# Interleaving the output projection with half of the first feed-forward column group, and loading the residual rows two tiles ahead

## The chip, the core and the metric

The kernel runs on one core of a Trainium2 chip. A core has a matrix engine (PE, whose weight loads are listed as PEld), a vector engine (DVE), a scalar engine (ACT), a general engine (POOL) and a sequencer that mostly issues transfers (SP). Each engine works through its own list of instructions in order; engines wait for each other by semaphores. Transfers (DMA) are issued from SP, ACT or POOL and share 16 DMA engines. The metric is the device time of one execution in microseconds (us). Before the change it is 2557.62 us, the median of three runs (2555.13 to 2560.41).

## The reference

One encoder layer over 2048 tokens of width 1024, in float32: a normed input goes through one input projection, half of the result through dilated attention and half through a gated unit, and then:

```python
    mix = jnp.concatenate([attn, sgu], axis=-1) @ w_out
    x = x + rms_norm(mix, g_post_mix)
    h = rms_norm(x, g_pre_ffn)
    f = jnp.square(jax.nn.relu(h @ w_ff1)) @ w_ff2
    return x + rms_norm(f, g_post_ffn)
```

`w_out` is 1024 x 1024, `w_ff1` 1024 x 4096, `w_ff2` 4096 x 1024. The change lies where the product with `w_out` ends and the feed-forward part begins.

## The kernel before, in words

Each float32 operand is split into a high and a low part (`split_sbuf`, L53, `split_psum`, L73), and each product is three matmuls of 128 x 128 by 128 x 512 that accumulate in one PSUM bank (`mm3`, L82: lines L84, L85, L86). Stage 1 is the input projection, stage 2 the attention with the gated unit's matmuls as filler on PE, and stage 3 the rest. The gated half of `w_out` is multiplied in stage 2 already; its product lies in DRAM as `part`. What is left for stage 3 is the attention half of `w_out`, whose pieces (`c.wo`, 8 pieces of 128 x 512) fill all 8 buffers of the weight pool `c.wp` when stage 2 ends.

Stage 3 begins with the output projection, a loop over 16 tiles of 128 tokens (L923). For tile i:

- `operand` (L889): the attention output `fa` and its reciprocal denominators `fr` (two transfers, each spread over 64 partitions) are loaded by SP, multiplied on POOL (L900), and split on ACT and DVE (L59, L60) into `mh` and `ml`. Operands are asked for two tiles ahead.
- `rest` (L904): the residual rows `r` (from `part`, 512 KB, L907) and `xt` (from x, 512 KB, L909), one tile ahead. There are 3 buffers for `r` and 2 for `xt`.
- 24 matmuls into two banks `mo` (L933), each added to its half of `r` by DVE (L938).
- `post` (L912): the mean square of `r` on ACT (L853) and POOL (L90, L91), the gain on DVE (L914), `xt` added on DVE (L915), and `r` stored to DRAM as `x1d` by a transfer that ACT issues (L916).
- for tiles 0 to 7, one tile later, `prep` (L858): the mean square again, `r` normed **in place** on ACT (L865), 8 transposes on PE into `tp` (L872, tile i's are called tp(i) below), and the split of these into `hh` and `hl` (L75, L76), the operand h of the feed-forward part for tokens 0 to 1023.

Norming `r` in place overwrites what the store of `x1d` reads, so L865 waits until that transfer has landed. On ACT's list the store of tile i+1 stands behind the norming of tile i.

Then comes the feed-forward part, in two halves of 1024 tokens, each with 8 groups of 512 columns of `w_ff1`. `ff1` (L961) takes a group in two passes of 96 matmuls (4 banks `f`, 8 row blocks of weights, 3 matmuls each), squares the result and splits it into `fh` and `fl`; `ff2` (L985) multiplies by 512 rows of `w_ff2` (banks `g`). The first group's `w_ff1` pieces are asked for in tile 15 (L936), since `c.wp` is taken by `c.wo` until then.

Order: the program is written as the loops say, and a scheduler then sets the order of each engine's list by its own priorities. Stage 2's PE and ACT lists are fixed by hand (`in_order`, L35). Pools that begin in stage 3 lie where pools of stage 2 lay; a tile in such a place waits for the last reader and writer of what was there. The pools `s3o` and `s3m` of the output projection are on the right side of the memory, where stage 2 had first its query and key tiles (free early) and next to them the pool `fk`, which is used until the last `w_out` piece is split and the last rows of `part` (tile `ot`, L712, stored by L713) have gone out.

## Time and profile before

| what | value |
| --- | --- |
| time, median of 3 runs | 2557.62 us |
| time of the profiled execution | 2554.44 us |
| its span, first to last instruction | 2552.5 us |
| PE busy | 2398.6 us, 94% of the span |
| DVE, ACT, POOL busy | 1071.2, 935.1, 506.7 us |
| mean granted TensorE clock, share of full speed | 0.972 |
| first matmul of the output projection | 1000.44 us |
| first matmul of the first ff2 (bank g) | 1182.20 us |

The profiled execution is 3.18 us below the median and lies 0.69 us under the lowest of the three runs; 1.94 us of it lie outside the span. Times below are us from the span's start. PE's busy share counts a matmul's whole length, and matmuls overlap, so how far PE is ahead is read from the start times of consecutive ones. Of the idle time before an instruction the profile names what ended it. A transfer is listed where it is issued; "to landing" is the time from there until its semaphore.

### The profile page before, as it was taken

The numbers are of one execution on the slowest core, as the hardware profiler recorded it, in microseconds if no ns is written. First come the engines' busy times: TensorE is split into PE (matmuls) and PEld (weight loads), VectorE is DVE, ScalarE is ACT, GpSimd is POOL, SyncE is SP. The second block draws the span as 40 slices with busy tenths as digits, with TensorE's granted clock in tenths as the row PEclk, the third lists the DMA queues.
The fourth block names the chain that finished last, engine by engine and source line by source line (L and its number), as shares of the span: only waits on it lengthen the run. The fifth ranks groups of instructions, "written<-read, shape, count | busy, mean of one in ns | idle before, by whom it ended". The sixth has DMA issues, their size and how long they took to land.

```text
span 2552.5 us, 31514 instructions
## 1 busy us (share of the span) xinstructions
PE 2398.6 (94%) x11591; PEld 2004.2 (79%) x11591; DVE 1071.2 (42%) x2246; ACT 935.1 (37%) x2053; POOL 506.7 (20%) x553
## 2 busy tenths in 40 slices
PE   8999999888799896689999999999999999999998
PEld 6787887677687785568888888888788888888887
DVE  5524523466666554562223323332731332233325
ACT  4424422366667573433312221222632122112212
POOL 4103103434333222431100100110210011001101
PEclk9999999998899898899999999999999999999999
DMA  7635465667767555772112111111521111111113
GB/s 275 223 121 193 149 173 173 169 161 169 186 173 179 142 154 168 218 260 91 50 34 66 46 50 38 58 46 49 181 93 46 41 54 50 46 50 50 50 42 124
DMA packets 221054, 296.14 MB, mean 116 GB/s; under 512 B 37089, under 2 KB 128740, under 8 KB 217828
## 3 DMA queue, kind: packets, MB, share of 16 engines
q1 hardware_dynamic: 214724, 273.15, 36.5%
q10 hardware_dynamic: 4640, 16.79, 1.7%
q0 software_dynamic: 1536, 4.20, 0.6%
q8 instruction: 91, 1.49, 0.2%
q14 instruction: 63, 0.52, 0.1%
HBM read 216.04 MB, written 78.55 MB: 115 GB/s over the span
## 4 chain that ended last, share of the span: by engine, by line
PE 73%; DMA 14%; DVE 4%; POOL 3%; ACT 3%; issue 2%; SPq 1%; POOLq 0%; DVEq 0%; ACTq 0%
PE f L84 10%; PE f L85 10%; PE f L86 10%; PE g L86 8%; PE g L84 8%; PE g L85 8%; PE mm L85 3%; PE mm L86 3%; PE mm L84 3%; DMA od<-lo 2%; DMA r<-part 2%; DMA lo<-acc 2%; PE t L588 1%; DMA v<-vd 1%; DMA x1d<-r 1%
## 5 line engine op out<-in xcount | busy, mean ns | idle before, releaser
L85 PE MATMUL f<-hh,wl 128*128 128x512 f32 x1024 | 398.5, 389 | 1.9 <-DVE wl L57 1.9
L84 PE MATMUL g<-wl,fh 128*128 128x512 f32 x1024 | 399.0, 390 | 0.0
L85 PE MATMUL g<-wh,fl 128*128 128x512 f32 x1024 | 398.6, 389 | 0.0
L86 PE MATMUL g<-wh,fh 128*128 128x512 f32 x1024 | 398.5, 389 | 0.0
L86 PE MATMUL f<-hh,wh 128*128 128x512 f32 x1024 | 398.4, 389 | 0.0
L84 PE MATMUL f<-hl,wh 128*128 128x512 f32 x1024 | 398.3, 389 | 0.0
L981 POOL TENSOR_TENSOR sq<-sq 128x512 f32<-128x512 f32 x128 | 132.1, 1053 | 1159.7 <-ACT sq L980 1159.7
L56 ACT ACTIVATE wh<-wraw,gain 128x512 fp32r<-128x512 f32 x200 | 143.3, 724 | 504.3 <-PE g L86 423.1
L57 DVE SCALAR_TENSOR_TENSOR wl<-wraw,gain,wh 128x512 fp32r<-128x512 f32 x200 | 157.9, 797 | 267.5 <-ACT wh L56 266.8
L60 DVE TENSOR_TENSOR fl<-sq,fh 128x512 fp32r<-128x512 f32 x128 | 99.1, 775 | 394.8 <-ACT fh L59 386.0
L85 PEld LDWEIGHTS f<-hh,wl 128*128 128x128 f32 x1024 | 192.3, 188 | 42.2 <-DVE wl L57 2.3
L84 PEld LDWEIGHTS f<-hl,wh 128*128 128x128 f32 x1024 | 192.3, 188 | 39.9
L86 PEld LDWEIGHTS g<-wh,fh 128*128 128x128 f32 x1024 | 192.3, 188 | 39.8
L86 PEld LDWEIGHTS f<-hh,wh 128*128 128x128 f32 x1024 | 192.3, 188 | 39.8
L85 PEld LDWEIGHTS g<-wh,fl 128*128 128x128 f32 x1024 | 192.3, 188 | 39.6
L84 PEld LDWEIGHTS g<-wl,fh 128*128 128x128 f32 x1024 | 192.3, 188 | 39.6
L1008 DVE TENSOR_TENSOR acc<-g,acc 128x512 f32<-128x512 f32 x192 | 127.3, 688 | 165.0 <-PE g L86 165.0
L577 ACT ACTIVATE p<-p,m 128x256 f32<-128x256 f32 (+2 forms) x384 | 173.9, 459 | 19.3 <-DVE m L549 19.3
L980 ACT ACTIVATE sq<-f 128x512 f32<-128x512 f32 x128 | 74.8, 597 | 289.2 <-PE f L86 281.9
L60 DVE TENSOR_TENSOR wl<-wraw,wh 128x512 fp32r<-128x512 f32 x144 | 101.8, 708 | 171.2 <-ACT wh L59 169.9
L59 ACT CAST wh<-wraw 128x512 fp32r<-128x512 f32 x144 | 89.5, 622 | 189.2 <-PE f L86 173.5
L525 DVE CUSTOM_DVE_ANT_0 p<-s,bias 128x256 f32<-128x256 f32 (+2 forms) x384 | 120.9, 355 | 42.7 <-PE s L509 32.0
(157 smaller groups left out, 4223.5 us busy)
## 6 DMA issues: line engine op xcount, KB each, us to landing
wraw<-in_w_ff_dram SPq DMA_DIRECT2D x256, 256.0 KB, 2.7
wraw<-in_w_in_dram SPq DMA_DIRECT2D x72, 256.0 KB, 2.7
xt<-in_x_dram SPq DMA_DIRECT2D x32, 512.0 KB, 5.4
v<-vd SPq DMA_DIRECT2D x40, 256.0 KB, 7.0
v<-vd SPq DMA_DIRECT2D x8, 1088.0 KB, 7.9
hd<-ht ACTq DMA_DIRECT2D x16, 512.0 KB, 5.1
vd<-vt SPq DMA_DIRECT2D x16, 512.0 KB, 3.1
qd<-e SPq DMA_DIRECT2D x32, 256.0 KB, 2.8
```

What stands on the lines that cost most here:

```text
L56: nc.scalar.activation(hi, src, AF.Copy, scale=scale)
L57: nc.vector.scalar_tensor_tensor(lo, src, scale, f32(hi), ALU.mult, ALU.subtract)
L59: nc.scalar.copy(hi, src)
L60: nc.vector.tensor_tensor(lo, src, f32(hi), ALU.subtract)
L84: nc.tensor.matmul(out, lhsT=lh, rhs=rl, start=start, stop=False)
L85: nc.tensor.matmul(out, lhsT=ll, rhs=rh, start=False, stop=False)
L86: nc.tensor.matmul(out, lhsT=lh, rhs=rh, start=False, stop=stop)
L525: nc.vector.tensor_tensor_reduce(po, so, bo, -1.0, 1e38, ALU.add, ALU.min, o.nm[:, br, cc:cc + 1])
L577: nc.scalar.activation(p[:, at + lo:at + hi], p[:, at + lo:at + hi], AF.Exp, bias=o.m[:, br, cc:cc + 1], scale=-1.0, accum_out=o.dn[:, br, ...
L980: nc.scalar.activation(sq, b, AF.Relu)
L981: nc.gpsimd.tensor_tensor(sq, sq, sq, ALU.mult)
L1008: nc.vector.tensor_tensor(av, b, av, ALU.add)
```

## The change

The first group of the feed-forward part for tokens 0 to 1023 is cut in two column halves of 256. The first half's 96 matmuls are done in two units of 48, one for tokens 0 to 511 (asked for from tile 5 on) and one for tokens 512 to 1023 (from tile 9 on), put between the matmuls of the output projection. Their weights are loaded as pieces of 128 x 256 into tiles of their own (`first`), the first 8 in tiles 1 to 4, those of the second half in tiles 13 to 15. The second half's 96 matmuls follow the loop, as before.

Beside this: `r` has 4 buffers and `xt` 3, and both are asked for two tiles ahead; the pool of `r` moves to the right side; the gain rows `gmix` and `gpost` share one buffer, so that `gpost` is loaded behind the loop; the tiles `fh` and `fl` lie in two pools of 2 instead of one of 5; `post` is no longer held back for the last three tiles; the first `w_ff2` pieces (`load2(0)`) are asked for behind the loop.

```diff
-        gpost = bcast_row(nc, cst, a["g_post_ffn"][0:1], D, "gpost")
...
+        fpa = ctx.enter_context(tc.tile_pool(name="s3f", bufs=2))
+
+        def ff1_unit(h, ws, c0, es, fs, pool):
+
+            hh, hl = h
+            bs = [pm.tile([P, 512], F32, name=f"f{m}", tag="mm3") for m in range(2 * len(es))]
+            for kc in range(8):
+                wh, wl = ws[kc]
+                for m, b in enumerate(bs):
+                    k, e = divmod(m, len(es))
+                    cs = slice(c0 + k * P, c0 + (k + 1) * P)
+                    ts = slice(es[e] * 512, (es[e] + 1) * 512)
+                    mm3(nc, b, wh[:, cs], wl[:, cs], hh[:, kc, ts], hl[:, kc, ts], kc == 0, kc == 7)
+                yield
+            for k in range(2):
+                if len(fs) == k:
+                    fs.append(tuple(pool.tile([P, 1024], F32R, name=x, tag=x) for x in ("fh", "fl")))
+                fh, fl = fs[k]
+                for e in range(len(es)):
+                    ts = slice(es[e] * 512, (es[e] + 1) * 512)
+                    sq = wk.tile([P, 512], F32, name="sq", tag="sq")
+                    nc.scalar.activation(sq, bs[k * len(es) + e], AF.Relu)
+                    nc.gpsimd.tensor_tensor(sq, sq, sq, ALU.mult)
+                    split_sbuf(nc, sq, fh[:, ts], fl[:, ts])
...
-            op = octx.enter_context(tc.tile_pool(name="s3o", bufs=1, side="right"))
-            om = octx.enter_context(tc.tile_pool(name="s3m", bufs=3, side="right"))
-            orp = octx.enter_context(tc.tile_pool(name="s3r", bufs=3))
-            gmix = bcast_row(nc, op, a["g_post_mix"][0:1], D, "gmix")
+            op = octx.enter_context(tc.tile_pool(name="s3o", bufs=8, side="right"))
+            rctx = octx.enter_context(ExitStack())
+            om = rctx.enter_context(tc.tile_pool(name="s3m", bufs=3, side="right"))
+            orp = rctx.enter_context(tc.tile_pool(name="s3r", bufs=4, side="right"))
+            gmix = bcast_row(nc, cst, a["g_post_mix"][0:1], D, "gmix", "gain")
+
+            def first(kc, pr):
+
+                raw = wk.tile([P, 512], F32, name="wraw", tag="wraw", bufs=c.nraw)[:, 0:256]
+                nc.sync.dma_start(raw, w1[kc * P:(kc + 1) * P, pr * 256:(pr + 1) * 256])
+                wh = op.tile([P, 256], F32R, name="w1h", tag="w1h")
+                wl = op.tile([P, 256], F32R, name="w1l", tag="w1l")
+                split_sbuf(nc, raw, wh, wl, c.gffn[:, kc:kc + 1])
+                return wh, wl
...
-                xt = wk.tile([P, D], F32, name="xt3", tag="xt3")
+                xt = wk.tile([P, D], F32, name="xt3", tag="xt3", bufs=3)
...
-            rx = [rest(0)]
-            old = []
+            rx = [rest(i) for i in range(near)]
+            old, wa, wb, fs0 = [], [], [], []
             for i in range(16):
                 if i + ahead < 16:
                     ops.append(operand(i + ahead))
-                if i + 1 < 16:
-                    rx.append(rest(i + 1))
+                if i + near < 16:
+                    rx.append(rest(i + near))
+                if 1 <= i < 5:
+                    wa += [first(kc, 0) for kc in range(2 * i - 2, 2 * i)]
                 (mh, ml), (r, xt) = ops.pop(0), rx.pop(0)
+                if i in (5, 9):
+                    unit = ff1_unit(h, wa, 0, (i // 9,), fs0, fpa)
+                steps = {5: 3, 6: 3, 7: 3, 9: 2, 10: 2, 11: 2, 12: 3}.get(i, 0)
                 for n in range(2):
...
                     nc.vector.tensor_tensor(r[:, ns], b, r[:, ns], ALU.add)
-                late.append((i, r, xt))
-                if i < 13:
-                    post(*late.pop())
+                    for _ in range((steps + 1 - n) // 2):
+                        next(unit, None)
+                post(i, r, xt)
...
+                if i >= 13:
+                    wb += [first(kc, 1) for kc in range(len(wb), (3, 6, 8)[i - 13])]
+            rctx.close()
+            v0 = load2(0)
+            fpb = ctx.enter_context(tc.tile_pool(name="s3g", bufs=2))
+            fs1 = []
+            for _ in ff1_unit(h, wb, 0, (0, 1), fs1, fpb):
+                pass
+
+        gpost = bcast_row(nc, cst, a["g_post_ffn"][0:1], D, "gpost", "gain")
```

What this does to the order on the engines is shown at three places; the number behind a tile's name tells it from others of that name. First SP's list where stage 2 ends and stage 3 begins, before the change: `od` is the attention output in DRAM, `rd` the denominators, `wraw` a raw piece of `w_out`, `ot` the last rows of `part`.

```order
L894 DMA fa_10020<-od_90 128x4x128
L713 DMA part_87<-ot_9812 128x512
L894 DMA fa_10030<-od_90 128x4x128
L894 DMA fa_10044<-od_90 128x4x128
...
L66 DMA wraw_9961<-in_w_out_dram 128x512
L897 DMA fr_10021<-rd_91 64x4x128
L897 DMA fr_10031<-rd_91 64x4x128
L897 DMA fr_10045<-rd_91 64x4x128
L909 DMA xt3_10056<-in_x_dram 128x1024
L713 DMA part_87<-ot_9967 128x512
L907 DMA r_10040<-part_87 128x1024
L907 DMA r_10054<-part_87 128x1024
```

Here the loads of the first three `fa` stand among the last transfers of stage 2, and the second halves of the first three `fr` directly behind the last `w_out` piece. The same place after the change:

```order
L66 DMA wraw_9961<-in_w_out_dram 128x512
L946 DMA xt3_10047<-in_x_dram 128x1024
L946 DMA xt3_10061<-in_x_dram 128x1024
L713 DMA part_87<-ot_9967 128x512
L920 DMA wraw_10114<-in_w_ff1_dram 128x256
L920 DMA wraw_10204<-in_w_ff1_dram 128x256
L931 DMA fa_10021<-od_90 128x4x128
L934 DMA fr_10022<-rd_91 64x4x128
L931 DMA fa_10031<-od_90 128x4x128
L934 DMA fr_10032<-rd_91 64x4x128
L944 DMA r_10041<-part_87 128x1024
L944 DMA r_10045<-part_87 128x1024
```

(Of four `w_ff1` pieces and of two transfers for each `fr`, one or two rows stand.) All loads of `fa` and `fr` are now behind the last store of `part` and behind four `w_ff1` pieces. The semaphores of `fa_10021` name the landing of that last store, the split of `wraw_9961` on DVE and the last matmul of stage 2's filler: the tile lies where the pool `fk` was.

Last, PE's list from the transposes of tile 2 to those of tile 3 after the change, with the first rows of the first feed-forward unit (`f0`, `f1`) behind them:

```order
L871 MATMUL tp3_10338<-ident_58,r_10059 128x128 x4
L871 MATMUL tp3_10345<-ident_58,r_10059 128x128 x4
L85 MATMUL mo_10450<-wh_9914,ml_10274 128x512
L86 MATMUL mo_10450<-wh_9923,mh_10273 128x512
L871 MATMUL tp3_10422<-ident_58,r_10110 128x128 x4
L871 MATMUL tp3_10429<-ident_58,r_10110 128x128 x4
L84 MATMUL f0_10464<-hl3_10006,w1h_10116 128x512
L85 MATMUL f0_10464<-hh3_10005,w1l_10117 128x512
L84 MATMUL f1_10465<-hl3_10006,w1h_10116 128x512
```

(Of the five matmuls of `mo_10450` between the two, the first and the last stand.) Before, 28 matmuls of `mo` stood between these two groups of transposes. From here to the transposes of tile 7 the list has all 48 matmuls of the first unit; behind those of tile 7 it has 156 of `mo` (129 before) and all 48 of the second unit; the 96 of the second column half follow. The number of PE instructions is the same as before, and from the first ff2 on the lists of PE are the same.

## Rows read from the trace of the kernel before

**Rows 1.** By stretch: us; PE, PEld, DVE, ACT, POOL busy; granted clock; DMA share; GB/s.

```profile
1030.00:1106.00 76.00, 56.93 (x244) 45.49 (x243) 42.15 (x51) 35.48 (x57) 32.48 (x37) 0.85 0.74 217
1106.00:1139.00 33.00, 31.11 (x136) 24.80 (x134) 22.48 (x27) 10.48 (x18) 7.44 (x12) 1.00 0.86 295
1139.00:1182.00 43.00, 43.00 (x191) 35.58 (x191) 19.09 (x25) 20.14 (x33) 12.29 (x13) 1.00 0.49 159
```

**Rows 2.** PE's waits, 940 to 1145 us: total, times, longest.

```profile
PE tp L872 <- ACT r L865: 28.8, 7, 9.7
PE mo L84 <- ACT mh L59: 19.9, 1, 19.9
PE f L85 <- DVE wl L57: 1.9, 1, 1.9
```

**Rows 3.** PE in order of time: start, length, instruction, idle before.

```profile
1000.44 0.79 PE L84 MATMUL mo<-wl,mh 128*128 128x512 f32 x1 [19.86 <-ACT mh L59]
...
1029.62 1.97 PE L872 MATMUL tp<-ident,r 128*128 128x128 f32 x8 [9.73 <-ACT r L865]
...
1105.35 1.10 PE L872 MATMUL tp<-ident,r 128*128 128x128 f32 x8 [0.39 <-ACT r L865]
1106.20 0.48 PE L84 MATMUL mo<-wl,mh 128*128 128x512 f32 x1
...
1136.49 0.40 PE L84 MATMUL f<-hl,wh 128*128 128x512 f32 x1
...
1179.71 0.39 PE L85 MATMUL f<-hh,wl 128*128 128x512 f32 x1
...
1182.20 0.39 PE L84 MATMUL g<-wl,fh 128*128 128x512 f32 x1
```

**Rows 4.** SP's issues at the start: start, length, transfer.

```profile
989.32 1.54 SPq L66 DMA_DIRECT2D wraw<-in_w_out_dram  x3
990.96 1.96 SPq L897 DMA_DIRECT2D fr<-rd  x3
...
995.71 0.33 SPq L713 DMA_DIRECT2D part<-ot  x1
```

**Rows 5.** POOL in order of time, the first operand.

```profile
998.49 1.25 POOL L900 TENSOR_TENSOR fa<-fa,fr 128x512 f32<-128x512 f32 x1 [5.19 <-DMA fr<-rd]
```

**Rows 6.** Issue to landing of a whole line: first `part` (L713), then `fr` (L897).

```profile
DMA to landing us min/median/max: 2.0/4.7/9.1
...
DMA to landing us min/median/max: 5.0/9.1/11.3
```

**Rows 7.** ACT in order of time: norming (L865), stores issued (L916).

```profile
1051.62 1.15 ACT L865 ACTIVATE r<-r,rs 128x1024 f32<-128x1024 f32 x1 [8.22 <-DMA x1d<-r]
1053.97 0.33 ACTq L916 DMA_DIRECT2D x1d<-r  x1
...
1070.21 1.15 ACT L865 ACTIVATE r<-r,rs 128x1024 f32<-128x1024 f32 x1 [2.56 <-DMA x1d<-r]
1072.37 0.36 ACTq L916 DMA_DIRECT2D x1d<-r  x1
...
1093.58 1.15 ACT L865 ACTIVATE r<-r,rs 128x1024 f32<-128x1024 f32 x1 [7.81 <-DMA x1d<-r]
1096.61 0.35 ACTq L916 DMA_DIRECT2D x1d<-r  x1
```

**Rows 8.** Chain that ended last, 1060 to 1106 us, by line.

```profile
by line: DMA r<-part 72.9%; DMA x1d<-r 25.6%; DVE r L915 7.6%; DVE r L938 4.7%; ACT hh L75 2.8%; ACT r L865 2.5%; issue 2.5%; PE tp L872 1.5%; ACTq L916 0.8%; SPq L909 0.7%; DVEq L938 0.2%; ACTq L865 0.1%; SPq L907 0.1%
```

**Rows 9.** DVE's waits, 1000 to 1140 us.

```profile
DVE r L938 <- DMA r<-part: 30.5, 11, 8.6
```

**Rows 10.** ACT in order of time: the splits behind the first transposes.

```profile
1030.77 0.59 ACT L75 CAST hh<-tp 128x512 fp32r<-128x512 f32 x1 [0.69 <-PE tp L872]
```

**Rows 11.** Transfers issued 1000 to 1060 us, then 1106 to 1139: KB, median to landing.

```profile
x1d<-r ACTq DMA_DIRECT2D x4, 512.0 KB, 7.9
...
x1d<-r ACTq DMA_DIRECT2D x4, 512.0 KB, 3.4
```

More of the change, by code (lines that the diff above doesn't have):

```diff
@@ L91, in rstd_pow, with bcast_row @@
     nc.gpsimd.tensor_tensor(out, out, c.mhalf[:, 0:1], ALU.pow)
-def bcast_row(nc, pool, row, n, name):
-    t = pool.tile([P, n], F32, name=name, tag=name, bufs=1)
+def bcast_row(nc, pool, row, n, name, tag=None):
+    t = pool.tile([P, n], F32, name=name, tag=tag or name, bufs=1)
     nc.sync.dma_start(t, row.partition_broadcast(P))
@@ new lines, in load2 @@
+        def load2(g):
+            return [[piece(nc, c, w2[(4 * g + k) * P:(4 * g + k + 1) * P, n * 512:(n + 1) * 512]) for k in range(4)]
+                    for n in range(2)]
+        with ExitStack() as octx:
+            op = octx.enter_context(tc.tile_pool(name="s3o", bufs=8, side="right"))
[10 more added lines that the diff above has]
+                return wh, wl
@@ L916, in post @@
                 nc.scalar.dma_start(x1d[i // 8][(i % 8) * P:(i % 8 + 1) * P, :], r)
-            ahead, behind = 2, 1
-            late = []
+            ahead, near, behind = 2, 2, 1
             ops = [operand(i) for i in range(ahead)]
-            rx = [rest(0)]
-            old = []
+            rx = [rest(i) for i in range(near)]
+            old, wa, wb, fs0 = [], [], [], []
             for i in range(16):
@@ L945, in stage3 @@
                     old.append((r, h[0], h[1], i))
-            for x in late:
-                post(*x)
+                if i >= 13:
[7 more added lines that the diff above has]
+        gpost = bcast_row(nc, cst, a["g_post_ffn"][0:1], D, "gpost", "gain")
         with ExitStack() as fctx:
-            fp = fctx.enter_context(tc.tile_pool(name="s3f", bufs=5))
-            ap_ = fctx.enter_context(tc.tile_pool(name="s3a", bufs=1))
+            ap_ = fctx.enter_context(tc.tile_pool(name="s3a", bufs=1, side="right"))
             def load1(g):
@@ L955, in load1 @@
                         for kc in range(8)]
-            def load2(g):
-                return [[piece(nc, c, w2[(4 * g + k) * P:(4 * g + k + 1) * P, n * 512:(n + 1) * 512]) for k in range(4)]
-                        for n in range(2)]
             def ff1(h, ws):
-                hh, hl = h
                 fs = []
-                for pr in range(2):
-                    bs = [pm.tile([P, 512], F32, name=f"f{m}", tag="mm3") for m in range(4)]
-                    for kc in range(8):
-                        wh, wl = ws[kc]
-                        for m in range(4):
-                            cs = slice((2 * pr + m // 2) * P, (2 * pr + m // 2 + 1) * P)
-                            ts = slice((m % 2) * 512, (m % 2 + 1) * 512)
-                            mm3(nc, bs[m], wh[:, cs], wl[:, cs], hh[:, kc, ts], hl[:, kc, ts], kc == 0, kc == 7)
-                    for k in range(2):
-                        fh = fp.tile([P, 1024], F32R, name="fh", tag="fh")
-                        fl = fp.tile([P, 1024], F32R, name="fl", tag="fl")
-                        fs.append((fh, fl))
-                        for e in range(2):
-                            b = bs[2 * k + e]
-                            ts = slice(e * 512, (e + 1) * 512)
-                            sq = wk.tile([P, 512], F32, name="sq", tag="sq")
-                            nc.scalar.activation(sq, b, AF.Relu)
-                            nc.gpsimd.tensor_tensor(sq, sq, sq, ALU.mult)
-                            split_sbuf(nc, sq, fh[:, ts], fl[:, ts])
+                for pr, pool in enumerate((fpa, fpb)):
+                    two = []
+                    for _ in ff1_unit(h, ws, 2 * pr * P, (0, 1), two, pool):
+                        pass
+                    fs += two
                 return fs
@@ L1010, in stage3 @@
             NG = FF // 512
-            ws = w1s
+            ws = None
             for half in range(2):
@@ L1015, in done @@
                 def done(i, bs):
-                    x1 = wk.tile([P, D], F32, name="xf", tag="xt3")
+                    x1 = wk.tile([P, D], F32, name="xf", tag="xt3", bufs=3)
                     rows = slice(i * P, (i + 1) * P)
@@ L1021, in done @@
                     ms = sm.tile([P, 2], F32, name="ms4", tag="ms4")
-                    y = wk.tile([P, D], F32, name="y", tag="y", bufs=1)
+                    y = ap_.tile([P, D], F32, name="y", tag="y", bufs=1)
                     for n, b in enumerate(bs):
@@ L1041, in next_in @@
                 def next_in(i):
-                    x1 = wk.tile([P, D], F32, name="xp", tag="xp", bufs=2)
+                    x1 = ap_.tile([P, D], F32, name="xp", tag="xp", bufs=2)
                     nc.sync.dma_start(x1, x1d[1][i * P:(i + 1) * P, :])
@@ L1048, in stage3 @@
                 for g in range(NG):
-                    v = load2(g)
-                    fs = ff1(h, ws)
+                    v, fs = (v0, fs0 + fs1) if half == g == 0 else (load2(g), ff1(h, ws))
                     last = g == NG - 1
```

5 lines of the change are left out of this document (removed).

## The prediction

> **What bounds the kernel now.** I read the busy shares by stretch first, then PE's waits, then PE in order of time around them, and last the chain of waits with ACT's and SP's lists in the stretch that PE loses. By stretch [rows 1], PE is full from 1139 us on, and it is from there to the end of the feed-forward part that most of the span lies; nothing of the change touches that. What is left is the output projection, from the first `mo` matmul at 1000.44 to the first `ff2` matmul at 1182.20 [rows 3]. PE's waits there are few kinds [rows 2]: 19.9 us ahead of the first `mo`, 28.8 us in 7 waits of the transposes for the normed `r`, and 1.9 us of the first feed-forward matmuls for a split weight. In order of time [rows 3] the transposes' waits all lie between tp(0) at 1029.62 and tp(7) at 1105.35, where the granted clock averages 0.85 [rows 1]; behind tp(7) PE runs on without a gap but the 1.9 us. So the stretch has three parts: up to tp(0), from tp(0) to tp(7) (75.7 us, 10.8 a tile), and behind tp(7) (76.85 us).
>
> What paces the middle part is seen on the chain [rows 8]: 72.9% of the stretch shown is the load of `r`, 25.6% the store `x1d`. ACT's list [rows 7] shows a second loop of nearly the same length: norming a tile waits for its own store to land, the next store stands behind that norming, and a store takes 7.9 us in the median there [rows 11].
>
> **The change part by part.**
>
> *The pitch of PE.* From 1106.20 to 1136.49 there are 129 `mo` matmuls, 0.2348 us each; from 1179.71 to 1182.20, 11 of `f`, 0.2264 us each [rows 3]. The change adds no matmul; it moves 48 of `f` ahead of tp(7) and, by the order of PE's list, 27 of `mo` from ahead of tp(7) to behind it. The other 48 of `f` in the loop stand behind tp(7), where PE had no gap to fill. What is covered by waits is thus 48 x 0.2264 = 10.9 us less 27 x 0.2348 = 6.3 us: 4.6 us, not the 21.7 us of all 96.
>
> *Behind tp(7).* Transposes 0.85 (1105.35 to 1106.20), a wait of 1.5 for tile 7's split, which the second unit now needs at once (two ACT splits of 0.59 [rows 10] and DVE's behind them), 156 x 0.2348 = 36.6, 144 x 0.2264 = 32.6, and 0.5 for the first weight or a bank of the second column half (between 0 and the 1.9 of before): 72.0 us against 76.85. So the first `ff2` matmul is as late as before when tp(7) comes at 1110.2.
>
> *The start.* Before, SP issued the `fr` loads at 990.96, right behind the last `w_out` pieces, and POOL had its first operand at 998.49 [rows 4, 5], 7.5 us later; the first `mo` followed 1.95 us behind that. Now these loads stand behind the last store of `part`, which SP cannot issue before 995.71 since it waits for ACT's copy, behind four `w_ff1` pieces (4 x 0.51 by the three `wraw` of 1.54 us [rows 4], so until 998.1), and `fa` waits for that store to land as well: 2.0 us at least, 4.7 in the median [rows 6], so 997.7 to 1000.4. I take 999. Two more issues at 0.65 each [rows 4] and a landing of 7.5 us as before (5.0 to 11.3 by [rows 6]), then the 1.95: first `mo` at 1009.8, 9.4 us late. With both ends it is 1006.3 to 1015. Behind the waiting `fa` on SP are all `fr`, the first `r` and every later operand, so nothing else can start PE.
>
> *tp(0).* Before, it came 29.2 us after the first `mo`, of which PE worked all but the wait of 9.7, so 19.5 [rows 3]. The rest was the post-processing of tile 0, held on POOL by operands that waited for `fr`. Now three operands stand ahead of its mean square on POOL instead of four, and its `r` is there in time; the bounds are 19.5 and 29.2, I take about the middle, 24.2. tp(0) at 1034.0, 4.4 us later than before: half of the late start is paid back out of the 9.7 us wait.
>
> *tp(0) to tp(7).* Four buffers and a load two tiles ahead take the load of `r` off the loop: a load now has one more tile's time to land, and DVE no longer stands at L938 (30.5 us in 11 waits [rows 9]) with L915 and the store behind it. What is late next is the other loop, store, landing, norming, next store, which nothing in the change shortens. So I count only what the store lost to the `r` wait after the norming ahead of it had ended [rows 7]: 1052.77 to 1053.97, 1071.36 to 1072.37, 1094.73 to 1096.61, 4.1 us in three tiles. Over seven I take 6, near this lower end; the upper end is what PE itself needs, 155 x 0.2348 + 48 x 0.2264 + 7 x 0.85 = 53.3 of the 75.7 us, a gain of 22. Below nothing it can go too: the matmuls of the unit stand ahead of `mo` and make posts later, up to some 5 us. The first unit costs another 1.5 us wait for tile 3's split, as above. The 48 `f` matmuls lie beside the waits as long as the loop takes over 53.3 us. Result: 75.7 - 6 + 1.5 = 71.2, tp(7) at 1105.2.
>
> *The rest.* The squaring and splits of the two units fall into ACT's and POOL's gaps; `w_ff1` brings 0.5 MB between tp(0) and tp(7), where before 1 MB of it was loaded, so no more bytes; `gpost` and the first `w_ff2` pieces move behind the loop, under 21.7 us of matmuls of the second column half. `fh`, `fl` in two pools of 2 are free long before the next group needs them, 96 matmuls behind `ff2`. I cost these at nothing; if the `w_ff2` pieces came late, the first `ff2` would wait, and 2 us is what it would cost by the one such wait of before.
>
> *Sum.* 1105.2 + 72.0 = 1177.2 against 1182.20: 5.0 us less. Against the profiled execution of 2554.44 that is 2549.4; since that execution was 3.18 under the median, the forecast on the median's scale is 2557.62 - 5.0 = 2552.6.
>
> **The length of a store.** The rows have 7.9 us in the median while `fr` loads run and 3.4 us behind them, for the same 512 KB [rows 11]. The Trainium skill, "DMA: Bandwidth & Descriptors", section "Anatomy of one DMA — SWDGE (gpsimd) path", fits a transfer as about 2.0 us fixed and its bytes at 436 GB/s, which would be 3.2 us here, an estimate by that page. The trace agrees behind tp(7) and not ahead of it. A store of that length would put the loop under PE's own pace; this is rival A.
>
> **The rivals.**
>
> A, *PE sets the pace.* With `r` out of the way fewer transfers collide, and a store takes nearer 3.4 to 5 than 7.9 us. Then tiles 1 to 3 take 8 us each (store 5, norming 1.15, the rest transposes and issues), 24 in all, and from tp(3) on PE's own list sets the pace: 96 `mo` x 0.2348 = 22.5, 48 `f` x 0.2264 = 10.9, four groups of transposes 3.4 and the 1.5 us wait make 38.3, some 40 with tile 7's store at its end. tp(7) at 1034 + 24 + 40 = 1098, the end at 1170, 12 us less: 2545.4, and 2538 with a tp(0) 7 us earlier, by the early ends of the start. For it: the 3.4 us behind tp(7) at a DMA share of 0.86 [rows 1, 11], higher than the 0.74 of the middle part. Against it: `fr` is loaded in the middle part as before, and it is there that stores are long.
>
> B, *the late first operand is not paid back.* `fa` waits for the store of `part` and `fr` lands late, the first `mo` is at 1015, and the chain to tp(0) keeps its 29.2 us; the loop of stores keeps its 75.7. tp(7) at 1044.2 + 75.7 + 1.5 = 1121.4, the end at 1193.4, 11.2 us more: 2568.8; with half of it, 2562. It decides from tp(7) at 1110.2 on. For it: the load is in fact queued behind all that stage 2 leaves, and one store loop was already nearly as long as the `r` loop. Against it: the 9.7 us wait at tp(0) is there to be used.
>
> C, *all 96 matmuls go into waits*: the end 21.7 us earlier, 2536. Against it, half of them stand where PE has no gap. The Trainium skill's page "Perfetto Trace Analysis", section "Optimization Strategy", says that a kernel whose regimes have different busiest engines can gain by interleaving them, and so points this way; the trace agrees for the part up to tp(7) alone.
>
> **How the numbers follow.** The forecast has 0.45, with its own range 2547 to 2558 (first `mo` 3 us either way, 4 to 9 us for the loop). A has 0.27, B 0.23, C 0.05. This measurement cannot tell less than 0.2%, 5.1 us, from no change. Faster by more: A, C and somewhat under half of the forecast's range, 0.27 + 0.05 + 0.18 = 0.50. Slower by more: most of B, 0.19. The rest, 0.31, is no change. The range that leaves out 2 in 10 cuts C and the far end of A below and the far end of B above: 2537 to 2567.
>
> **What would show it.** In the profile after: the first `mo` near 1010, its wait ended by an operand whose `fr` landed late (right: start); L938 waiting far less than 30.5 us for `r` (right: buffers); norming still ended by `x1d` landings and 9.5 to 10.5 us a tile between tp(0) and tp(3) (right: the store is the loop that is left); the waits of transposes smaller behind tp(3), since matmuls of `f` stand there; no gap behind tp(7). I am wrong if tp(7) comes ahead of 1098 or behind 1112, if norming no longer waits for stores, or if a wait shows up behind 1182 for `w_ff2` or a bank.

## The result and the profile after

The changed kernel takes 2570.28 us in the median of 5 runs (2565.18 to 2575.23), against 2557.62 us before. The ratio is 1.0051, 95% interval [1.0034, 1.0068]: 12.7 us slower, clear of what this measurement can tell from no change, and outside the range of 2537 to 2567 us. The profiled execution (2569.82 us, span 2567.6) stands close to the median. One run each of two later kernels, e12 (2745.15 us) and e13 (2744.01 us), had a granted clock of 0.84 instead of 0.97 and is left out of their medians and ratios.

PE's waits between 940 and 1145 us answer to [rows 2]. The transposes wait longer than before (28.8 us there), although 48 `f` matmuls now stand between them.

```profile
PE tp L871 <- ACT r L864: 36.0, 7, 11.5
PE mo L84 <- ACT mh L59: 29.4, 3, 28.1
PE f L84 <- DVE hl L76: 1.5, 2, 1.0
```

PE in order of time answers to [rows 3]: first `mo`, tp(0), tp(3), the first unit's first `f`, the `mo` behind twelve of these, tp(4), tp(7), the second unit's first `f`, and the first `ff2`.

```profile
1002.28 0.79 PE L84 MATMUL mo<-wl,mh 128*128 128x512 f32 x1 [28.10 <-ACT mh L59]
...
1034.74 1.97 PE L871 MATMUL tp<-ident,r 128*128 128x128 f32 x8 [10.19 <-ACT r L864]
...
1068.45 1.97 PE L871 MATMUL tp<-ident,r 128*128 128x128 f32 x8 [11.52 <-ACT r L864]
1070.96 0.80 PE L84 MATMUL f<-hl,w1h 128*128 128x512 f32 x1 [0.55 <-DVE hl L76]
...
1075.30 0.40 PE L84 MATMUL mo<-wl,mh 128*128 128x512 f32 x1
...
1085.38 1.09 PE L871 MATMUL tp<-ident,r 128*128 128x128 f32 x8 [2.42 <-ACT r L864]
...
1123.42 1.09 PE L871 MATMUL tp<-ident,r 128*128 128x128 f32 x8 [2.89 <-ACT r L864]
1125.47 0.79 PE L84 MATMUL f<-hl,w1h 128*128 128x512 f32 x1 [0.96 <-DVE hl L76]
...
1197.33 0.40 PE L84 MATMUL g<-wl,fh 128*128 128x512 f32 x1
```

The first `ff2` matmul is 15.1 us later than before, and so is the end of the span: the loss lies wholly ahead of it. From tp(3) to tp(7) the kernel takes 55.0 us instead of 43.2. That is not idle time of PE: the transposes' waits from tp(4) to tp(7) come to 2.42, 2.42, 3.62 and 2.89 us. PE works, but on `f`, while the next tile's chain has not begun.

By stretch, as [rows 1], the two in which the time goes:

```profile
1030.00:1106.00 76.00, 51.44 (x221) 41.04 (x222) 35.97 (x46) 32.59 (x54) 28.88 (x35) 0.84 0.68 184
1106.00:1139.00 33.00, 25.52 (x100) 20.09 (x99) 18.58 (x23) 13.61 (x23) 9.59 (x13) 0.84 0.56 182
```

PE does fewer instructions in both than before (221 for 244, 100 for 136), and the transfers move less, 184 GB/s for 217: there is no engine that has become full. (The second stretch lay behind tp(7) before, where PE had hardly a wait; now tp(7) is at 1123.42, and the loop fills half of it; its granted clock is 0.84, where it was 1.00.)

SP's issues around the start answer to [rows 4].

```profile
988.38 0.33 SPq L713 DMA_DIRECT2D part<-ot  x1
988.75 1.89 SPq L920 DMA_DIRECT2D wraw<-in_w_ff_dram  x4
991.20 0.38 SPq L931 DMA_DIRECT2D fa<-od  x1
991.62 1.30 SPq L934 DMA_DIRECT2D fr<-rd  x2
...
998.57 5.15 SPq L931 DMA_DIRECT2D fa<-od  x1
```

The operands' loads follow the last store of `part` and the `w_ff1` pieces, and the first `mo` comes 13.9 us behind that store, where it was 4.7 before. But the store itself is 7.3 us earlier in this execution (988.38 against 995.71), so the first `mo` is only 1.8 us late.

POOL's waits for operands, 1000 to 1140 us, before and then after (total, times, longest):

```profile
POOL fa L900 <- DMA fr<-rd: 37.1, 8, 9.2
...
POOL fa L900 <- DMA fa<-od: 14.5, 4, 4.4
```

```profile
POOL fa L937 <- DMA fr<-rd: 57.4, 10, 16.0
...
POOL fa L937 <- DMA fa<-od: 21.6, 5, 7.7
```

DVE's 30.5 us of waits for `r` [rows 9] are gone without a rest; POOL's waits for the operands have grown by 27.4 us in the same stretch. How such a wait reaches a transpose is seen ahead of tp(0), all engines in order of time:

```profile
1025.40 1.06 ACT L852 ACTIVATE jk<-r 128x1024 bf16<-128x1024 f32 x1 [1.41 <-DVE r L975]
1028.93 1.26 POOL L937 TENSOR_TENSOR fa<-fa,fr 128x512 f32<-128x512 f32 x1 [5.59 <-DMA fr<-rd]
1030.23 0.62 ACT L59 CAST mh<-fa 128x512 fp32r<-128x512 f32 x1 [3.68 <-POOL fa L937]
1030.28 0.22 POOL L90 TENSOR_SCALAR rs<-ms 128x1 f32<-128x1 f32 x1
...
1030.75 1.05 ACT L852 ACTIVATE jk<-r 128x1024 bf16<-128x1024 f32 x1
...
1033.54 1.15 ACT L864 ACTIVATE r<-r,rs 128x1024 f32<-128x1024 f32 x1 [1.64 <-POOL rs L91]
```

The multiply of a later tile waits 5.59 us for `fr`. Behind it on POOL's list stands the mean square whose sum ACT had ready at 1026.5; behind the split on ACT's list stands the mean square of the norming (1030.75) that tp(0) waits for.

Last, one tile of the loop between tp(4) and tp(5), again all engines:

```profile
1091.23 0.39 PE L86 MATMUL mo<-wh,mh 128*128 128x512 f32 x1
...
1091.66 0.69 DVE L975 TENSOR_TENSOR r<-mo,r 128x512 f32<-128x512 f32 x1 [3.68 <-PE mo L86]
...
1092.39 1.06 ACT L852 ACTIVATE jk<-r 128x1024 bf16<-128x1024 f32 x1
...
1093.57 1.06 ACT L852 ACTIVATE jk<-r 128x1024 bf16<-128x1024 f32 x1
...
1094.81 1.09 POOL L90 TENSOR_SCALAR rs<-ms 128x1 f32<-128x1 f32 x1 [0.31 <-ACT jk L852]
...
1095.98 1.52 POOL L91 TENSOR_TENSOR rs<-rs,mhalf 128x1 f32<-128x1 f32 x1
...
1097.53 1.15 ACT L864 ACTIVATE r<-r,rs 128x1024 f32<-128x1024 f32 x1 [2.81 <-POOL rs L91]
```

From the end of a tile's last `mo` (1091.62) to the next transposes (1098.73) is 7.1 us of chain: DVE's addition, two mean squares on ACT, POOL, the norming. The second mean square is that of the tile before, which the transposes are of; it stands behind the first, tile i's, only because `post` is written ahead of `prep`. Behind tp(4) PE has 10 `f`, 12 `mo`, 6 `f`, 12 `mo`, 2 `f`. The 10 `f` (1086.23 to 1088.65, 2.4 us) are ahead of the `mo` with which the chain begins, so they lengthen the loop; only the last 8 `f` and the 12 `mo` among them lie beside the 7.1 us.

The loop's excess can be added up from PE's list. Behind tp(3), tp(4) and tp(5) stand 12, 10 and 10 `f` ahead of that `mo`; they take 4.3 us (1070.96 to 1075.30, the first seven at half the pace, behind a wait of 11.52 us), 2.4 and 2.4. Behind tp(5) the first unit's result is split as well, and on DVE's list one split stands ahead of the addition that the chain begins with:

```profile
1105.57 1.69 DVE L60 TENSOR_TENSOR fl<-sq,fh 128x512 fp32r<-128x512 f32 x2 [4.24 <-ACT fh L59]
...
1107.18 0.68 DVE L975 TENSOR_TENSOR r<-mo,r 128x512 f32<-128x512 f32 x1
```

The last `mo` of that tile began at 1104.59. An addition that follows its `mo` at once, as at 1091.66, would have begun 2.2 us sooner. That makes 11.3 us, of the 11.8 by which tp(3) to tp(7) is longer than before. (Before, waits for `r` held the same stretch, so that the two agree so closely is in part chance.)

### The profile page after: what moved, and what is told of

It is laid out like the page before. It is cut to its first block, busy times and chain, and to the rows that moved or that the text cites. A ratio compares the mean times of both kernels' runs of the same rounds, so it can differ in the third digit from the quotient of the medians.

```text
span 2567.6 us, 31563 instructions
## 1 busy us (share of the span) xinstructions
PE 2401.3 (94%) x11591; PEld 2004.3 (78%) x11591; DVE 1070.2 (42%) x2254; ACT 935.5 (36%) x2061; POOL 495.5 (19%) x553
## 4 chain that ended last, share of the span: by engine, by line
PE 53%; DVE 1%; ACT 1%; POOL 1%; issue 0%; DMA 0%; DVEq 0%; POOLq 0%; ACTq 0%
PE f L84 9%; PE f L86 9%; PE f L85 9%; PE g L86 8%; PE g L85 8%; PE g L84 8%; DVE xf L1058 1%; PE mo L86 1%; PE mo L84 0%; PE mo L85 0%; ACT jk L1051 0%; DVE acc L1050 0%; PE tp L871 0%; ACT jk L852 0%; DMA xp<-x1d 0%
## 5 line engine op out<-in xcount | busy, mean ns | idle before, releaser
L84 PE MATMUL f<-hl,wh 128*128 128x512 f32 x960 | 373.7, 389 | 0.0
L86 PE MATMUL f<-hh,wh 128*128 128x512 f32 x960 | 373.7, 389 | 0.0
L85 PE MATMUL f<-hh,wl 128*128 128x512 f32 x960 | 373.7, 389 | 0.0
L56 ACT ACTIVATE wh<-wraw,gain 128x512 fp32r<-128x512 f32 x192 | 137.7, 724 | 502.8 <-PE g L86 421.8
L57 DVE SCALAR_TENSOR_TENSOR wl<-wraw,gain,wh 128x512 fp32r<-128x512 f32 x192 | 152.0, 798 | 269.7 <-ACT wh L56 269.1
L86 PEld LDWEIGHTS f<-hh,wh 128*128 128x128 f32 x960 | 180.3, 188 | 37.4
L85 PEld LDWEIGHTS f<-hh,wl 128*128 128x128 f32 x960 | 180.3, 188 | 37.3
L84 PEld LDWEIGHTS f<-hl,wh 128*128 128x128 f32 x960 | 180.3, 188 | 37.3
```

Of the source, the lines that this page charges most:

```text
L56: nc.scalar.activation(hi, src, AF.Copy, scale=scale)
L57: nc.vector.scalar_tensor_tensor(lo, src, scale, f32(hi), ALU.mult, ALU.subtract)
L84: nc.tensor.matmul(out, lhsT=lh, rhs=rl, start=start, stop=False)
L85: nc.tensor.matmul(out, lhsT=ll, rhs=rh, start=False, stop=False)
L86: nc.tensor.matmul(out, lhsT=lh, rhs=rh, start=False, stop=stop)
```

## The experiments

The table has, from one profiled execution of each kernel, the lengths in us of the five stretches: last store of `part` to first `mo`, to tp(0), to tp(3), to tp(7), to the first `ff2`. The ratio is that of the times, against runs of the kernel before on the same chip, with its interval. How far a stretch varies from one execution of a kernel to the next is not known from one; tp(0) to tp(3) lies anywhere from 32.7 to 38.7 in e1, e3, e5, e6 and e8, all with the same loads of operands, so a few us there say little, and the ratios are firmer.

| kernel | to mo | to tp(0) | to tp(3) | to tp(7) | to ff2 | ratio |
| --- | --- | --- | --- | --- | --- | --- |
| before | 4.7 | 29.2 | 32.5 | 43.2 | 76.9 | 1 |
| after | 13.9 | 32.5 | 33.7 | 55.0 | 73.9 | 1.0051 [1.0034, 1.0068] |
| e1 operands' place | 4.6 | 25.5 | 35.7 | 54.8 | 74.8 | 1.0023 [1.0010, 1.0036] |
| e2 prep first | 14.1 | 28.4 | 45.1 | 53.2 | 77.6 | 1.0080 [1.0060, 1.0100] |
| e3 units later | 14.1 | 32.4 | 35.4 | 40.2 | 76.6 | 1.0010 [0.9994, 1.0026] |
| e4 r one ahead | 15.2 | 33.8 | 33.1 | 56.2 | 74.8 | 1.0060 [1.0042, 1.0078] |
| e5 = e1 + e3 | 4.0 | 26.4 | 38.3 | 40.5 | 79.0 | 0.9986 [0.9973, 0.9999] |
| e6 before, r two ahead | 4.6 | 24.0 | 38.7 | 43.2 | 82.4 | 1.0005 [0.9991, 1.0018] |
| e7 fr once | 16.0 | 24.3 | 23.2 | 53.8 | 75.1 | 0.9981 [0.9964, 0.9997] |
| e8 = e5 + norm elsewhere | 3.5 | 26.1 | 32.7 | 43.3 | 78.5 | 0.9978 [0.9964, 0.9993] |
| e9 = e8 + pair loads | 3.8 | 22.0 | 31.3 | 37.4 | 75.4 | 0.9932 [0.9915, 0.9948] |
| e10 = e2 + norm elsewhere | 13.4 | 26.2 | 48.8 | 52.3 | 77.4 | 1.0104 [1.0085, 1.0124] |
| e11 before, pair loads | 2.8 | 23.3 | 28.8 | 37.8 | 77.7 | 0.9925 [0.9909, 0.9942] |
| e12 after, pair loads | 15.9 | 23.4 | 33.0 | 54.4 | 73.8 | 1.0023 [1.0007, 1.0038] |
| e13 = e12 + prep first | 15.8 | 21.9 | 29.3 | 50.2 | 75.2 | 0.9986 [0.9970, 1.0001] |
| e14 = e13 + norm elsewhere | 16.8 | 19.6 | 37.1 | 45.0 | 75.8 | 0.9990 [0.9976, 1.0003] |

**e1, the operands' place.** The pool of the operands is taken first again:

```
+om = octx.enter_context(tc.tile_pool(name="s3m", bufs=3, side="right"))
 op = octx.enter_context(tc.tile_pool(name="s3o", bufs=8, side="right"))
 rctx = octx.enter_context(ExitStack())
-om = rctx.enter_context(tc.tile_pool(name="s3m", bufs=3, side="right"))
```

> The changed kernel with one thing undone: the pool of the operands (fa, fr, mh, ml) is taken first on the right side of the memory, so that it lies where it lay before the change and its first loads need not wait for the last store of part. Theory (the transposes from tp(3) on wait for a chain of posts that PE's f matmuls delay): only the start moves; the first mo comes 4 to 8 us behind the last store of part instead of 13.9, tp(0) to tp(3) some 5 to 9 us earlier, tp(3) to tp(7) stays near 55 us; time 2561 to 2566. Rival (late operand loads pace the whole loop): tp(3) to tp(7) falls to about 43 us as before the change; time near 2550.

2564.26 us. The first `mo` is again 4.6 us behind the last store, and tp(0) comes 7.0 us sooner behind the first `mo`; tp(3) to tp(7) stays at 54.8. So the place costs the start and nothing behind tp(3). The last store of `part` is back at 995.08 us, though, 6.7 us later than in the changed kernel: part of the gain is given back in stage 2 (last section).

**e2, prep first.** The two lines are swapped:

```
+if len(old) == behind:
+    prep(*old.pop(0))
 post(i, r, xt)
-if len(old) == behind:
-    prep(*old.pop(0))
```

> The changed kernel with two program lines swapped: the norming of tile i-1 (prep) is written ahead of the post-processing of tile i (post), so that on ACT and POOL its mean square no longer stands behind that of tile i. Theory (the transposes wait for tile i's matmuls only by the order of these two lists): tp(3) to tp(7) falls from 55 us to about 40 (96 mo, 48 f and the transposes on PE), the waits of the transposes from 36 us to under 20; time 2553 to 2560. Rival (operand loads pace the loop): tp(3) to tp(7) stays over 50 us, time within 4 us of 2570.

2578.28 us: a miss. tp(3) to tp(7) fell by 1.8 us only, and the stretch ahead of it grew by 11.4. ACT's waits for a landing store, 7.0 us in two waits in the changed kernel, have become 18.2 us in six:

```profile
ACT r L864 <- DMA x1d<-r: 18.2, 6, 5.0
```

**e3, units later.** Both units stand behind tile 8:

```
-if i in (5, 9):
-    unit = ff1_unit(h, wa, 0, (i // 9,), fs0, fpa)
-steps = {5: 3, 6: 3, 7: 3, 9: 2, 10: 2, 11: 2, 12: 3}.get(i, 0)
+if i in (9, 12):
+    unit = ff1_unit(h, wa, 0, (i // 12,), fs0, fpa)
+steps = {9: 3, 10: 3, 11: 3, 12: 3, 13: 3, 14: 3}.get(i, 0)
```

> The changed kernel with both feed-forward units moved behind tile 8 (steps in tiles 9 to 14), so that PE has no f matmul between tp(3) and tp(6) and 13 ahead of tp(7). Theory (f matmuls ahead of mo lengthen the loop): tp(3) to tp(6) takes about 33 us as before the change instead of 45, tp(7) comes at 1108 to 1113; behind it 144 mo and 179 f, some 77 us; time 2557 to 2563. Rival (operand loads pace the loop, whatever PE does): tp(3) to tp(6) stays near 45 us, and the f matmuls now behind tp(7) are added: 2575 to 2580.

2558.24 us, as the theory had it. tp(3), tp(4), tp(5) and tp(6) of e3:

```profile
1065.57 1.97 PE L871 MATMUL tp<-ident,r 128*128 128x128 f32 x8 [5.85 <-ACT r L864]
1076.35 1.09 PE L871 MATMUL tp<-ident,r 128*128 128x128 f32 x8 [0.70 <-ACT r L864]
1086.59 1.97 PE L871 MATMUL tp<-ident,r 128*128 128x128 f32 x8 [5.40 <-ACT r L864]
1096.33 1.09 PE L871 MATMUL tp<-ident,r 128*128 128x128 f32 x8 [0.37 <-ACT r L864]
```

tp(3) to tp(6) is 30.8 us, against 44.8 in the changed kernel, and the stretch behind tp(7) grew by 2.7 only. POOL's waits for operands, 1000 to 1140 us, are still 62.6 us in sum (79.0 in the changed kernel, 51.6 before), so operands still came late while this stretch was as short as before.

**e4, r one tile ahead.** `near` is 1 and `r` has three buffers again.

> The changed kernel with the residual rows loaded one tile ahead again and three buffers for r (xt keeps three). Theory (r loads are not what paces the changed kernel): DVE waits again for r, some 10 us in all, but tp(7) moves by under 4 us; time 2567 to 2574. Rival (the two-tiles-ahead loads pay for part of the damage): 10 us or more slower, 2580.

2573.98 us, and tp(3) to tp(7) is 56.2. DVE's waits for `r` came back with 1.9 us, not 10: the loads two tiles ahead are worth little here.

**e5, both e1 and e3.**

> Both edits at once on the changed kernel: the operands' pool where it lay before, and both feed-forward units behind tile 8. Theory (two separate costs, the late first operand and the f matmuls ahead of mo): they add up; first mo 4 to 5 us behind the last store of part, tp(3) to tp(7) near 41 us, behind tp(7) 76; time 2550 to 2556, 4 us under the units alone and no slower than the kernel before. Rival (the earlier start is lost again in the loads that follow): the same time as the units alone, 2558.

2554.74 us. The costs add up, and the kernel is now level with the one before or a little under it. Of the change this leaves little: no `f` matmul fills a wait ahead of tp(6).

**e6, the kernel before with `r` and `xt` two tiles ahead, alone** (four and three buffers, both in the pool of `r`, which moves to the right side).

> The kernel before with one part of the change alone: four buffers for r, three for xt, both loaded two tiles ahead; no feed-forward matmul moved, operands where they were. Theory (what the r loads give up, the operand loads take: POOL's multiply waits for fr with the mean squares behind it): DVE's wait for r falls from 30.5 us to under 8, POOL's wait for operands grows over 52 us, tp(0) to tp(7) takes 70 to 76 us (75.7 before); time 2552 to 2557. Rival (the r ring was the loop): tp(0) to tp(7) near 62 us, time near 2543.

2558.24 us, no difference. DVE still waits 17.8 us for `r`, more than expected; POOL's waits for `fr` and `fa` are 45.4 us from 1000 us on (51.6 before), and from the first `mo` to tp(7) the DMA share is 0.77 at 212 GB/s (0.70 at 206 before). tp(0) to tp(7) took 82.0 us, where 70 to 76 was expected. So the `r` ring was not a loop that more buffers could open. That the operands take over was not shown by their waits here; that something other than buffers limits, is.

**e7, `fr` once.** Every tile uses the denominators of the first; the other tiles' loads of `fr` are left out. In `operand`:

```
-fr = om.tile([P, 4, P], F32, name="fr", tag="fr")
+fr = one[0] if one else om.tile([P, 4, P], F32, name="fr", tag="fr", bufs=1)
+one.append(fr)
...
-for e in range(2):
+for e in range(2 if i == 0 else 0):
```

> The changed kernel with the reciprocal denominators fr loaded for the first tile alone and used for all (left out: the other tiles' denominators, 30 transfers of 128 KB). Theory (fr loads hold POOL's list up to tp(3), the f matmuls ahead of mo from there on): tp(0) to tp(3) falls from 33.7 to 24 to 28 us, tp(3) to tp(7) stays over 48; time 2557 to 2564. Rival (operand loads pace the whole loop): tp(3) to tp(7) falls to near 40 as well, time near 2547. Second rival (neither): tp(0) to tp(3) stays near 33 us, time 2567 to 2571.

2555.45 us, 1.6 us under the expected range. tp(0) to tp(3) fell to 23.2 us, the shortest of all, and tp(3) to tp(7) stayed at 53.8. POOL's waits, 1000 to 1140 us:

```profile
POOL fa L940 <- DMA fr<-rd: 17.6, 1, 17.6
POOL fa L940 <- DMA fa<-od: 16.8, 10, 2.9
```

With no wait for an operand over 2.9 us (after the first one) the stretch with the `f` matmuls is as long as ever. This and e3 together show the two costs apart: loads of operands up to tp(3), the place of `f` behind it.

**e8, the norm in a tile of its own, on e5.**

```
-nc.scalar.activation(x1, x1, AF.Copy, scale=rs)
+nc.scalar.activation(x1 if xn is None else xn, x1, AF.Copy, scale=rs)
...
-old.append((r, h[0], h[1], i))
+old.append((r, orp.tile([P, D], F32, name="rn", tag="rn", bufs=2), h[0], h[1], i))
```

> The kernel with the operands' pool where it lay and the units behind tile 8, and in addition the norming of tiles 0 to 7 written into a tile of its own (two buffers), so that it no longer waits for the store of x1d to land. Theory (the store loop no longer paces once r comes two tiles ahead; operands and mean squares do): under 3 us less than without this edit. Rival (the forecast's loop, store, landing, norming, next store): tp(0) to tp(7) 8 us or more shorter than without it.

2552.31 us, ratio 0.9978 against 0.9986: no difference that the intervals show. No norming waits for a store any more; tp(0) to tp(7) is 76.0 us, against 78.8 in e5. The store loop of the forecast is not what paces e5.

**e9 and e11, pair loads.** `fa` and `fr` are loaded for two tiles at once, on e8 (with one buffer for the normed tile instead of two) and on the kernel before:

```
-sl = slice(i * P, (i + 1) * P)
-fa = om.tile([P, 4, P], F32, name="fa", tag="fa")
-fr = om.tile([P, 4, P], F32, name="fr", tag="fr")
+if i % 2 == 0:
+    sl = slice(i * P, (i + 2) * P)
+    fa2 = om.tile([P, 4, 2 * P], F32, name="fa", tag="fa", bufs=2)
+    fr2 = om.tile([P, 4, 2 * P], F32, name="fr", tag="fr", bufs=2)
...
+ps = slice(i % 2 * P, (i % 2 + 1) * P)
+fa, fr = pair[0][:, :, ps], pair[1][:, :, ps]
```

> The kernel with the operands' pool where it lay, the units behind tile 8 and the norm in a tile of its own (one buffer here), and in addition fa and fr loaded for two tiles at once: half as many transfers, of twice the size, in rows of 1 KB instead of 512 bytes, the same bytes. Theory (the loads of fr and fa hold POOL's list, and they are slow for their many short rows): tp(0) to tp(7) falls from 76 us to 62 to 70, time 2541 to 2549. Rival (the bytes count, not the rows): tp(0) to tp(7) 73 us or more, time 2550 to 2555.

> The kernel before with one edit that is no part of the change: fa and fr loaded for two tiles at once, in rows of 1 KB. Theory (short rows slow all transfers of the output projection, so the loop of r loads and stores too): tp(0) to tp(7) falls from 75.7 to 64 to 72 us, time 2545 to 2553. Rival (the bytes count): within 3 us of the kernel before.

2534.52 and 2533.24 us, against 2551.63 of the kernel before on the same chip: both faster than expected. From the first `mo` to tp(7), first before, then e11 (us; busy PE, PEld, DVE, ACT, POOL; granted clock; DMA share; GB/s):

```profile
1000.44:1105.35 104.91, 76.11 (x312) 60.18 (x312) 53.51 (x64) 42.78 (x68) 42.21 (x48) 0.85 0.70 206
```

```profile
988.54:1078.40 89.86, 77.71 (x313) 61.33 (x314) 53.99 (x65) 42.56 (x68) 42.40 (x49) 0.87 0.86 242
```

The transfers of these stretches, in all and as issued there, KB each and median us to landing, first before, then e11:

```profile
DMA packets 17861, 21.61 MB, mean 206 GB/s; under 512 B 1106, under 2 KB 13912, under 8 KB 17855
...
r<-part SPq DMA_DIRECT2D x10, 512.0 KB, 7.1
xt<-in_x_dram SPq DMA_DIRECT2D x9, 512.0 KB, 5.1
x1d<-r ACTq DMA_DIRECT2D x9, 512.0 KB, 7.9
fr<-rd SPq DMA_DIRECT2D x26, 128.0 KB, 10.2
```

```profile
DMA packets 10947, 21.75 MB, mean 242 GB/s; under 512 B 784, under 2 KB 6928, under 8 KB 10942
...
xt<-in_x_dram SPq DMA_DIRECT2D x10, 512.0 KB, 6.0
r<-part SPq DMA_DIRECT2D x9, 512.0 KB, 4.5
x1d<-r ACTq DMA_DIRECT2D x9, 512.0 KB, 6.7
...
fr<-rd SPq DMA_DIRECT2D x12, 256.0 KB, 8.1
```

About the same bytes move in fewer packets and in half as many operand loads: an `fr` transfer of twice the size lands sooner, and so do `r` and `x1d`, which were not touched; `xt`, not touched either, lands later. POOL's waits for `fr` and `fa` in these stretches fall from 48.1 to 14.9 us. That the length of the rows is the cause, as the theory had it, is not shown (last section). e9 holds what is left of the change and is no faster than e11, which has nothing of it. e11 has the lowest time of the study, with e9 too near to tell apart.

**e10, prep first and the norm elsewhere.**

> The changed kernel with prep of tile i-1 written ahead of post of tile i, which alone took tp(3) to tp(7) to 53 us and the whole to 2578, and in addition the norming written into a tile of its own. Theory (with prep first, a norming waits for the landing of a store that has only just been issued, 18.2 us in 6 waits; without that wait the swap does what was expected of it): those waits are gone, tp(3) to tp(7) takes 41 to 47 us, time 2560 to 2569. Rival (the store is not what held it, the operands are): tp(3) to tp(7) over 50 us, time 2573 to 2579.

2580.44 us, 1.4 us over the rival's range: without the waits for stores tp(3) to tp(7) is still 52.3. POOL waits 47.8 us for `fr` and 17.6 for `fa`, the longest 11.0; that with `prep` first the mean squares stand behind those multiplies is the likely reason, and was not tried by itself.

**e12, the changed kernel with pair loads,** and **e13, the same with prep first.**

> The changed kernel with fa and fr loaded for two tiles at once in rows of 1 KB, all else as in the change. Theory (two costs: the operand loads up to tp(3), the f matmuls ahead of mo from there on): tp(0) to tp(3) 24 to 29 us instead of 33.7, tp(3) to tp(7) stays 50 to 55; some 10 to 16 us faster than the changed kernel, 2549 to 2558, and 15 us or more slower than the kernel before with the same loads (2533). Rival (loads are the whole cost): tp(3) to tp(7) near 42 us, time within 5 us of 2533.

> The same with prep of tile i-1 written ahead of post of tile i. Theory (with the swap alone, late operands on POOL's list held the mean squares; now they come in time): tp(3) to tp(7) 40 to 47 us, 6 us or more faster than without the swap, 2540 to 2550. Rival (the f matmuls cost as much with either order of the posts): tp(3) to tp(7) over 50 us, time within 4 us of the run without the swap.

e12 takes 2561.06 us, 3 us over the expected range, at a ratio of 1.0023 where the kernel before gains to 0.9925: with the pair loads in both, the change costs about 0.98%, some 25 us, twice what it costs without them. tp(3) to tp(7) is 54.4 as expected; tp(0) to tp(3) at 33.0 is a miss, since tp(3) waits 11.9 us. e13 takes 2551.29 (2540 to 2550 expected), 9.8 us under e12 as expected, but tp(3) to tp(7) is 50.2, where 40 to 47 was expected. ACT's waits for stores in e13:

```profile
ACT r L864 <- DMA x1d<-r: 16.9, 6, 4.9
```

**e14, e13 with the norm elsewhere.**

> The changed kernel with fa and fr loaded for two tiles at once, prep of tile i-1 ahead of post of tile i, and the norming written into a tile of its own (one buffer). Theory (three loops of nearly one length lay over each other, operands, stores, and posts behind f matmuls; with the first two out of the way the swap frees the transposes from tile i's matmuls): no waits for x1d left, tp(3) to tp(7) 40 to 47 us, some 4 to 9 us faster than without the last edit, 2543 to 2549. Rival (the f matmuls cost as much with either order): tp(3) to tp(7) over 48 us, within 3 us of 2552.

tp(3) to tp(7) is 45.0 us: with one wait of 3.5 us for an operand in this stretch, none for the store, and the posts decoupled, the stretch is 7.2 us longer than e11's 37.8, where e12's is 16.6 longer. But the time, 2554.04 us, is as the rival had it: in the profiled execution tp(0) to tp(3) is 37.1 instead of 29.3. Why is not settled; the three edits help behind tp(3), and no kernel here has both a short first part and a short second one with the `f` matmuls inside.

## Why the prediction was wrong

Its sum, step by step, against the changed kernel's trace:

- **The start** was right in its mechanism and size: the first `mo` 14.1 us behind the last store of `part` by the forecast, 13.9 measured. What it missed is that the store came 7.3 us earlier, so that `mo` was only 1.8 us late.
- **tp(0)** came at 1034.74, forecast 1034.0, but by two errors that cancel: first `mo` 7.5 us early, and from there 32.5 us instead of 24.2. The mean squares of tile 0 and of its norming are held on POOL's and ACT's lists by late operands as before; that three multiplies and not four stand ahead of the first gained nothing. e7 shows what held it: with `fr` in time this takes 24.3.
- **tp(0) to tp(7)** is the step that failed: 71.2 us by the forecast, 88.7 measured, 17.5 of the 20.1 us by which the first `ff2` is later than forecast; tp(7) came at 1123.42, behind the 1112 that the prediction named as its own sign of being wrong. It said "What is late next is the other loop, store, landing, norming, next store". That loop is not what was late next: norming waits for stores 7.0 us in all (21.7 before), and e8 removes the wait without a gain that can be measured. Up to tp(3) the operand loads took over (e7). Behind it, "the matmuls of the unit stand ahead of `mo` and make posts later, up to some 5 us" named the mechanism, but only as a bound: the sum has nothing for it, and the bound is a third of what was measured. e3, which moves the units away, takes 14.8 us less there. The statement "The 48 `f` matmuls lie beside the waits as long as the loop takes over 53.3 us" counted PE's work against the loop's length, and did not ask which `f` stand between a tile's release and the `mo` that begins the next chain. By PE's list that could be read: 12, 10 and 10 of the 48 stand there, 32 in all, and they took 9.2 us. No run put the `f` behind that `mo` with all else equal; the order of `prep` and `post`, the other way to the same end, took the stretch to 53.2, 50.2 and 45.0 us (e2, e13, e14).
- **The load of `r`** off the loop: right that the wait goes, wrong that time goes with it. e6 and e4 find nothing for it.
- **The rest**, costed at nothing: the splits of the first unit's result held DVE's addition, and with it tp(6), for 2.2 us.
- **Behind tp(7)**: 72.0 forecast, 73.9 measured; the second unit's first matmuls go at half the pace (6 `f` in 2.7 us), behind 2.89 and 0.96 us of waiting.

Rival A had PE's own list set the pace from tp(3) on; it does lie in the loop, but as 55 us and not as 40, since only a part of it lies beside the chain of posts. C fell with it. Rival B had the sign and, with 2562 to 2568.8, nearly the size, but not the cause: its late start was paid back in part by stage 2, and its loop did not stay at 75.7. (Half of its 11.2 us would be 2563.2, not 2562.) No rival had as its cause the `f` ahead of `mo`, though PE's list was there to be read.

The section on the length of a store took 3.2 us from the Trainium skill, "DMA: Bandwidth & Descriptors". The fit given there is for transfers issued by gpsimd (POOL here), and this store is issued by ACT. From the first `mo` to tp(7) `x1d` takes 7.9 us in the median before, 6.3 in the changed kernel, 6.7 in e11 with pair loads, and 5.2 in e7 without most `fr` loads: what else is being loaded makes a part of the difference, and what the rest is stays open.

## What to carry to other kernels

Filler matmuls fill a wait only where they stand behind the last matmul of the chain that ends the wait; each one ahead of it lengthens the loop by its whole pitch. So read the filled engine's list from one release to the next, and count what stands ahead of the matmuls that begin the next chain. And when several loops of nearly one length lie over each other (here `r`, stores, operands, posts), opening one need not give anything (e6, e8); here one edit to the operands' loads gave 0.75% by itself (e11).

## What was not expected of the hardware

- Loading `fa` and `fr` for two tiles at once made the kernel 0.75% faster, but not by sparing the DMA engines work. From the first `mo` to tp(7) they moved 21.61 MB before and 21.75 in e11, and share times length is 73 us (0.70 of 104.91) and 77 us (0.86 of 89.86): they were as long at work, and idled less. The edit does more than lengthen the rows from 512 bytes to 1 KB. SP's issues of `fr` took 33.6 us for 26 transfers before and 8.8 us for 12 in e11, with other loads behind them on its list; and every second tile's operand is asked for one tile earlier, with room for four tiles instead of three. No run takes these apart. The Trainium skill, "DMA: Bandwidth & Descriptors", section "Specifications", gives 512 bytes as the smallest transfer that runs at line rate; by that, longer rows save the DMA engines nothing here, and their unchanged working time agrees. The Trainium skill's page "Perfetto Trace Analysis", section "DMA Optimizations", says that small transfers, under 2 KB, carry a noticeable cost each and should be put together; e9 and e11 are faster with theirs put together, but no run here shows such a cost at the DMA engines.
- Where the operands' loads stand among the last transfers of stage 2, its last store of `part` comes later: from a transfer just ahead of the first difference on SP's list (`yd`, issued at 903.18 us before, 899.92 after, 899.26 in e1) to that store it is 92.0 to 95.8 us in the seven kernels that have the operands' pool in its old place (92.5 before, 95.8 in e1), and 87.7 to 91.0 in the nine that have it in the new one (88.5 in the changed kernel). Through what the loads cost there was not tried. The other 3.3 us of the 7.3 were there already at 900 us, on equal lists of SP: over all profiled executions that transfer is issued between 889.79 and 903.85 us, which shows how far single executions drift apart.
- POOL's small instructions are not always small: L90 took 0.22 us at 1030.28 and 1.09 us at 1094.81, L91 0.58 and 1.52 us. The long ones fall beside DVE's instructions on whole tiles of `r`; that DVE is the cause was not tried.
